# The first k tile loaded as two column halves over the sync and the scalar hardware queue, the offsets moved to the scalar queue

## The chip, the cores and the metric

One core of a Trainium2 chip runs the kernel. The metric is the device time in microseconds (us), of which the profiled span, from the first to the last instruction, is about 1.6 us less. Lower is better.

Names: PE is TensorE, ACT ScalarE, DVE VectorE, POOL GpSimd, SP SyncE. "L53" is line 53 of a kernel's file. DMA queue q0 is POOL's (software descriptors), q1 is SP's and q10 is ACT's (both hardware).

## The reference

For each of 4 batches a window of 64 rows is cut from x at an offset known only at run time, and multiplied with one 4096 x 4096 matrix.

```python
B, S, D, W = 4, 4096, 4096, 64          # x: B,S,D  w: D,D  all float32; offsets: int64
for b in range(B):
    o = int(offsets[b])
    results.append(x[b, o:o+W] @ w)
return np.stack(results).astype(np.float32)
```

So 67.1 MB of w and 4.2 MB of x are read, and 4.2 MB written.

## The kernel before

All of w passes through SBUF once. A DMA issued by POOL reads float32 and writes float16 (`wh`). The first k tile (128 rows of w, 2 MB) goes another way: ACT loads it as float32 over a hardware queue and casts it itself, so that the DMA engines have work from ACT's issue at 0.87 us on, before POOL's first load is issued at 1.38 us. The offsets (32 bytes) come over SP; POOL reads them before it issues the four x loads.

```python
w0_32 = x_pool.tile([P, N], fp32, name="w0row")       # P = 128, N = 4096
w0_16 = x_pool.tile([P, N], fp16, name="w0half")
...
nc.sync.dma_start(out=off_t[:], in_=offsets[None, :])
nc.scalar.dma_start(out=w0_32[:], in_=w[0:P, :])
...
load(0, 1, 1)                                         # first wh tile, gpsimd queue, casts to fp16
make_identity(nc, identity[:])
for b in range(B):                                    # needs the offsets
    g, m = divmod(b, 2)
    o = nc.values_load(off_i32[0:1, 2 * b : 2 * b + 1], engines=[POOL], ...)
    nc.gpsimd.dma_start(out=x16[g][m * WIN : (m + 1) * WIN, :], in_=x[b][bass.ds(o, WIN), :])
for ng in range(n_ng):
    for ki in range(n_k):
        if (ng, ki) not in wh:
            load(ng, ki, 2 if ki < n_k - 4 - (ki % 2) else 1)

nc.scalar.copy(out=w0_16[:, :NG], in_=w0_32[:, :NG])  # NG = 2048
nc.scalar.copy(out=w0_16[:, NG:], in_=w0_32[:, NG:])
... # x transposed on PE; then, per column half, 32 k tiles x 2 row groups x 4 matmuls; results stored
```

Of the kernel before, what the change touches and what calls it, by code (L numbers as in the profile page):

```python
# [1 line left out]

# [5 lines left out]


@with_exitstack  # L10
def kernel(
    ctx: ExitStack,
    tc: tile.TileContext,
    x: bass.AP,
    w: bass.AP,
    offsets: bass.AP,
    out: bass.AP,
):
    nc = tc.nc
    fp32 = mybir.dt.float32  # L20
    fp16 = mybir.dt.float16

    B, S, D = x.shape
    _, N = w.shape
    WIN = out.shape[1]
    P = 128
    NT = 512
    NG = 2048
    n_k = D // P
    n_ng = N // NG  # L30
    n_sub = NG // NT
    G = B // 2

    POOL = mybir.EngineType.Pool

    const_pool = ctx.enter_context(tc.tile_pool(name="const", bufs=1))
    x_pool = ctx.enter_context(tc.tile_pool(name="xp", bufs=1))
    wh_pool = ctx.enter_context(tc.tile_pool(name="wh", bufs=12))
    st_pool = ctx.enter_context(tc.tile_pool(name="st", bufs=1))
    psum_pool = ctx.enter_context(tc.tile_pool(name="ps", bufs=1, space=bass.MemoryType.PSUM))  # L40

    identity = const_pool.tile([P, P], fp16, name="identity")
    off_t = const_pool.tile([1, B], mybir.dt.int64, name="off_t")
    w0_32 = x_pool.tile([P, N], fp32, name="w0row")
    w0_16 = x_pool.tile([P, N], fp16, name="w0half")
    x16 = [x_pool.tile([P, D], fp16, name=f"xrow{g}") for g in range(G)]
    xT = [x_pool.tile([P, D], fp16, name=f"xT{g}") for g in range(G)]
    ps = [psum_pool.tile([P, NT], fp32, name=f"bank{t}") for t in range(8)]

    ctx.enter_context(tc.manual_schedule())  # L50

    nc.sync.dma_start(out=off_t[:], in_=offsets[None, :])
    nc.scalar.dma_start(out=w0_32[:], in_=w[0:P, :])  # L53
    off_i32 = off_t.bitcast(mybir.dt.int32)

    def load(ng, ki, n):
        t = wh_pool.tile([P, n * NG], fp16, name="wh", tag="wh")
        nc.gpsimd.dma_start(  # L58
            out=t[:].rearrange("p (t n) -> p t n", t=n),
            in_=w[ki * P : (ki + n) * P, ng * NG : (ng + 1) * NG].rearrange(  # L60
                "(t p) n -> p t n", p=P
            ),
        )
        for i in range(n):
            wh[(ng, ki + i)] = t[:, i * NG : (i + 1) * NG]

    wh = {(ng, 0): w0_16[:, ng * NG : (ng + 1) * NG] for ng in range(n_ng)}
    load(0, 1, 1)
# [3 lines that stand above are left out]
        o = nc.values_load(  # L72
            off_i32[0:1, 2 * b : 2 * b + 1],
            engines=[POOL],
            min_val=0,
            max_val=S - WIN,
            skip_runtime_bounds_check_because="offsets are drawn below S - WIN",
        )
        nc.gpsimd.dma_start(  # L79
            out=x16[g][m * WIN : (m + 1) * WIN, :],  # L80
            in_=x[b][bass.ds(o, WIN), :]
# [6 lines that stand above are left out]
    nc.scalar.copy(out=w0_16[:, :NG], in_=w0_32[:, :NG])  # L88
    nc.scalar.copy(out=w0_16[:, NG:], in_=w0_32[:, NG:])  # L89
    for g in range(G):  # L90
        for t in range(8):
            for i in range(4):
                k = 4 * t + i
                nc.tensor.matmul(  # L94
                    out=ps[t][:, i * P : (i + 1) * P],
                    lhsT=x16[g][:, k * P : (k + 1) * P],
                    rhs=identity[:],
                    start=True,
                    stop=True,
                )  # L100
            dst = xT[g][:, t * NT : (t + 1) * NT]
            if t % 2 == 0:
                nc.vector.tensor_copy(out=dst, in_=ps[t][:])  # L103
            else:
                nc.scalar.copy(out=dst, in_=ps[t][:])  # L105

    def mm(g, j, ki, rhs, start, stop):
        nc.tensor.matmul(  # L108
            out=ps[4 * g + j][:],
            lhsT=xT[g][:, ki * P : (ki + 1) * P],  # L110
            rhs=rhs,
            start=start,
            stop=stop,
        )

    stage = [
        [st_pool.tile([P, NG], fp32, name=f"stage{ng}{g}") for g in range(G)]
        for ng in range(n_ng)
    ]
    q = [nc.scalar, nc.sync]  # L120
    for ng in range(n_ng):
        last = ng == n_ng - 1
        for ki in range(n_k):
            for g in range(G):
                for j in range(n_sub):
                    mm(g, j, ki, wh[(ng, ki)][:, j * NT : (j + 1) * NT], ki == 0, ki == n_k - 1)
        for j in range(n_sub):
            for g in range(G):
                dst = stage[ng][g][:, j * NT : (j + 1) * NT]
                if g == 0:  # L130
                    nc.scalar.copy(out=dst, in_=ps[4 * g + j][:])  # L131
                else:
                    nc.vector.tensor_copy(out=dst, in_=ps[4 * g + j][:])  # L133
        for g in range(G):
            (q[g] if last else nc.gpsimd).dma_start(  # L135
                out=out[2 * g : 2 * g + 2, :, ng * NG : (ng + 1) * NG],
                in_=stage[ng][g][:],
            )


# [1 line left out]
_INS = ['x', 'w', 'offsets']  # L142
_OUTS = [((4, 64, 4096), 'float32')]


# [23 lines left out]
```

## Time and profile before

| | before |
|---|---|
| device time, median of 6 runs | 183.55 us (183.4 to 183.72) |
| profiled span | 182.0 us |
| DMA time of the queues q0, q10, q1, as shares of 16 engines' span | 97.0 + 4.6 + 1.4 = 103% (the times of packets are added up, and packets of an engine can overlap) |
| HBM traffic over the span | 415 GB/s |
| PE busy | 67% |

The first extract is from the page of before: the DMA row of the 40 slices (tenths of busy time, 9 is 90% or more), the queues (packets, MB, share), the HBM bytes, and the shares of the chain that ended last.

```profile
DMA  5999999999999999999999999999999999999995
...
q0 software_dynamic: 9120, 36.70, 97.0%
q10 hardware_dynamic: 288, 3.15, 4.6%
q1 hardware_dynamic: 146, 1.05, 1.4%
...
HBM read 71.30 MB, written 4.19 MB: 415 GB/s over the span
...
DMA 88%; issue 3%; POOL 1%; DVE 1%; POOLq 1%; PE 1%; DVEq 0%
```

From the second slice to the last but one the DMA engines are busy 90% or more of the time, and the chain is nearly all weight stream. The next extract is from the view of waits (us in total, times, longest; "bank" is a PSUM tile that PE writes, and x is transposed at L94).

```profile
POOL wh L58 <- DMA wh<-in_w_dram: 105.8, 26, 5.8
...
PE bank L108 <- DMA wh<-in_w_dram: 32.7, 30, 1.9
...
PE bank L94 <- DMA xrow<-in_x_dram: 17.5, 2, 16.1
```

PE waits 32.7 us in 30 pieces for weights, and POOL waits 105.8 us for earlier loads to land before it may issue more. Both run behind the DMA engines. The third extract is the timeline (start, duration, instruction, idle before it and what ended it).

```profile
0.87 0.34 SPq L52 DMA_DIRECT2D off_t<-in_offsets_dram  x1
0.87 0.38 ACTq L53 DMA_DIRECT2D w0row<-in_w_dram  x1
...
1.38 0.66 POOL L58 DMA_DIRECT2D wh<-in_w_dram  x1 [0.81 <-POOLq L153]
...
3.54 0.53 POOL L79 DMA_DIRECT2D xrow<-in_x_dram  x1 [0.91 <-issue]
...
9.81 1.90 ACT L88 CAST w0half<-w0row 128x2048 f16<-128x2048 f32 x1 [7.25 <-DMA w0row<-in_w_dram]
...
11.62 1.89 ACT L89 CAST w0half<-w0row 128x2048 f16<-128x2048 f32 x1
...
16.07 3.57 PE L94 MATMUL bank<-identity,xrow 128*128 128x128 f16 x32 [16.07 <-DMA xrow<-in_x_dram]
...
24.41 1.92 PE L108 MATMUL bank<-w0half,xT 128*128 128x512 f16 x8
```

The things to see: the first DMAs are issued at 0.87 us; ACT casts the tile from 9.81 to 13.5 us; PE first uses it at 24.41 us. Between the tile and its use lie 10.9 us in which PE waits for x and then transposes it. Last, from the chain that ended last, the stretch in which the last weight tile lands (start, duration, what):

```profile
145.43 25.79 DMA wh<-in_w_dram
171.22 0.04 issue
```

The last weight tile lands at 171.22 us. What follows it takes 10.8 us to the end of the span: the last matmuls, their copies and the stores.

### The profile page before, as it was taken

The numbers are of one execution on the slowest core, as the hardware profiler recorded it, in microseconds if no ns is written. First come the engines' busy times: TensorE is split into PE (matmuls) and PEld (weight loads), VectorE is DVE, ScalarE is ACT, GpSimd is POOL, SyncE is SP. The second block draws the span as 40 slices with busy tenths as digits, with TensorE's granted clock in tenths as the row PEclk, the third lists the DMA queues.
The fourth block names the chain that finished last, engine by engine and source line by source line (L and its number), as shares of the span: only waits on it lengthen the run. The fifth ranks groups of instructions, "written<-read, shape, count | busy, mean of one in ns | idle before, by whom it ended". The sixth has DMA issues, their size and how long they took to land.

```text
span 182.0 us, 1329 instructions
## 1 busy us (share of the span) xinstructions
PE 122.8 (67%) x576; PEld 56.5 (31%) x576; DVE 10.5 (6%) x16; ACT 13.8 (8%) x19; POOL 27.7 (15%) x48
## 2 busy tenths in 40 slices
PE   0004699777777777777988777777777587799700
PEld 0004663333333322333433333333233232343300
DVE  0002540000000000000005000000000000000040
ACT  2081430000000000000004000000000000000210
POOL 4713310111111111110221111111111010100000
PEclk9999999999999999999999999999999999999995
DMA  5999999999999999999999999999999999999995
GB/s 180 348 217 216 206 214 215 216 214 215 212 213 212 216 215 216 214 215 210 212 214 217 215 215 214 212 214 213 215 216 214 215 215 211 214 212 216 367 398 216
DMA packets 9559, 40.97 MB, mean 225 GB/s; under 512 B 722, under 2 KB 722, under 8 KB 8658
## 3 DMA queue, kind: packets, MB, share of 16 engines
q0 software_dynamic: 9120, 36.70, 97.0%
q10 hardware_dynamic: 288, 3.15, 4.6%
q1 hardware_dynamic: 146, 1.05, 1.4%
q8 instruction: 4, 0.07, 0.1%
q14 instruction: 1, 0.01, 0.0%
HBM read 71.30 MB, written 4.19 MB: 415 GB/s over the span
## 4 chain that ended last, share of the span: by engine, by line
DMA 88%; issue 3%; POOL 1%; DVE 1%; POOLq 1%; PE 1%; DVEq 0%
DMA wh<-in_w_dram 88%; DVE stage L133 1%; POOL wh L58 1%; PE bank L108 1%; POOLq L72 1%; POOL xrow L79 0%; DVEq L164 0%; POOL identity masks.py:197 0%; POOLq L79 0%; POOLq L58 0%; POOLq masks.py:199 0%; POOLq L153 0%
## 5 line engine op out<-in xcount | busy, mean ns | idle before, releaser
L108 PE MATMUL bank<-wh,xT 128*128 128x512 f16 x496 | 112.0, 379 | 32.7 <-DMA wh<-in_w_dram 32.7
L108 PEld LDWEIGHTS <-xT 128*128 128x128 f16 x512 | 49.9, 98 | 98.5 <-issue 42.0
L58 POOL DMA_DIRECT2D wh<-in_w_dram x36 | 23.8, 662 | 116.8 <-DMA wh<-in_w_dram 105.8
L94 PE MATMUL bank<-identity,xrow 128*128 128x128 f16 x64 | 7.1, 311 | 17.5 <-DMA xrow<-in_x_dram 17.5
L131 ACT COPY stage<-bank 128x512 f32<-128x512 f32 x8 | 4.1, 599 | 144.4 <-PE bank L108 144.4
L133 DVE COPY stage<-bank 128x512 f32<-128x512 f32 x8 | 5.0, 682 | 145.1 <-PE bank L108 145.1
L94 PEld LDWEIGHTS <-xrow 128*128 128x128 f16 x64 | 6.7, 147 | 17.7 <-issue 17.7
L103 DVE CAST xT<-bank 128x512 f16<-128x512 f32 x8 | 5.5, 691 | 19.4 <-PE bank L94 19.4
L105 ACT CAST xT<-bank 128x512 f16<-128x512 f32 x8 | 4.7, 586 | 7.0 <-PE bank L94 7.0
L108 PE MATMUL bank<-w0half,xT 128*128 128x512 f16 x16 | 4.2, 380 | 0.2 <-DVE stage L133 0.2
L88 ACT CAST w0half<-w0row 128x2048 f16<-128x2048 f32 x1 | 1.9, 1897 | 7.2 <-DMA w0row<-in_w_dram 7.2
L79 POOL DMA_DIRECT2D xrow<-in_x_dram x4 | 2.1, 524 | 2.1 <-issue 2.1
L135 POOL DMA_DIRECT2D out_dram<-stage x2 | 1.1, 536 | 8.2 <-DMA wh<-in_w_dram 8.2
L89 ACT CAST w0half<-w0row 128x2048 f16<-128x2048 f32 x1 | 1.9, 1892 | 0.0
L88 ACT ACT_TABLE_LOAD x1 | 1.3, 1283 | 1.3 <-PEq L153 1.3
masks.py:199 POOL TENSOR_SCALAR_AFFINE_SELECT identity<-identity 128x128 f16<-128x128 f16 x1 | 0.3, 288 | 0.1
masks.py:197 POOL MEMSET identity<- 128x128 f16 x1 | 0.2, 223 | 0.0
L153 POOL MEMSET const-float32-0.0<- 128x1 f32 x1 | 0.1, 99 | 0.4 <-issue 0.4
L153 POOL MEMSET const-uint8-127<- 128x1 uint8 x1 | 0.1, 102 | 0.0
L153 POOL MEMSET const-bfloat16-1.0<- 128x1 bf16 x1 | 0.1, 101 | 0.0
L153 POOL MEMSET const-float32-1.0<- 128x1 f32 x1 | 0.1, 99 | 0.0
## 6 DMA issues: line engine op xcount, KB each, us to landing
wh<-in_w_dram POOLq DMA_DIRECT2D x26, 1024.0 KB, 36.6
wh<-in_w_dram POOLq DMA_DIRECT2D x10, 512.0 KB, 31.3
w0row<-in_w_dram ACTq DMA_DIRECT2D x1, 2048.0 KB, 8.9
xrow<-in_x_dram POOLq DMA_DIRECT2D x4, 512.0 KB, 12.2
out_dram<-stage POOLq DMA_DIRECT2D x2, 1024.0 KB, 22.8
out_dram<-stage ACTq DMA_DIRECT2D x1, 1024.0 KB, 4.9
out_dram<-stage SPq DMA_DIRECT2D x1, 1024.0 KB, 6.0
off_t<-in_offsets_dram SPq DMA_DIRECT2D x1, 0.0 KB
```

The source lines that it names most:

```text
L58: nc.gpsimd.dma_start(out=t[:].rearrange("p (t n) -> p t n", t=n), in_=w[ki * P : (ki + n) * P, ng * NG : (ng + 1) * NG].rearrange("(t p) ...
L72: o = nc.values_load(off_i32[0:1, 2 * b : 2 * b + 1], engines=[POOL], min_val=0, max_val=S - WIN, skip_runtime_bounds_check_because="offse ...
L79: nc.gpsimd.dma_start(out=x16[g][m * WIN : (m + 1) * WIN, :], in_=x[b][bass.ds(o, WIN), :])
L88: nc.scalar.copy(out=w0_16[:, :NG], in_=w0_32[:, :NG])
L89: nc.scalar.copy(out=w0_16[:, NG:], in_=w0_32[:, NG:])
L94: nc.tensor.matmul(out=ps[t][:, i * P : (i + 1) * P], lhsT=x16[g][:, k * P : (k + 1) * P], rhs=identity[:], start=True, stop=True,)
L103: nc.vector.tensor_copy(out=dst, in_=ps[t][:])
L105: nc.scalar.copy(out=dst, in_=ps[t][:])
L108: nc.tensor.matmul(out=ps[4 * g + j][:], lhsT=xT[g][:, ki * P : (ki + 1) * P], rhs=rhs, start=start, stop=stop,)
L131: nc.scalar.copy(out=dst, in_=ps[4 * g + j][:])
L133: nc.vector.tensor_copy(out=dst, in_=ps[4 * g + j][:])
L135: (q[g] if last else nc.gpsimd).dma_start(out=out[2 * g : 2 * g + 2, :, ng * NG : (ng + 1) * NG], in_=stage[ng][g][:],)
```

## The change

The intent is an earlier start: half of the first tile on each of two queues, so that the first half can be cast sooner, with rows of 8 KB instead of 16 KB. SP has to be free for its half, so the offsets move to ACT, ahead of ACT's half.

```diff
-    nc.sync.dma_start(out=off_t[:], in_=offsets[None, :])
-    nc.scalar.dma_start(out=w0_32[:], in_=w[0:P, :])
+    nc.sync.dma_start(out=w0_32[:, :NG], in_=w[0:P, :NG])
+    nc.scalar.dma_start(out=off_t[:], in_=offsets[None, :])
+    nc.scalar.dma_start(out=w0_32[:, NG:], in_=w[0:P, NG:])
```

## The prediction

> **What bounds the kernel now.** The DMA engines. In the page's slices the DMA row is at 9 (90% or more) from the second slice to the last but one; the queue table adds up to 103% of 16 engines' span; HBM moves 415 GB/s over the 182.0 us span. The chain that ended last is 88% "DMA wh<-in_w_dram", the weight stream on the gpsimd queue. PE waits 32.7 us for that stream. The Trainium skill (DMA: Bandwidth & Descriptors, Measured) lists 425 GB/s for a 16 MB load; this trace's 415 with start and tail included leaves little to gain by moving issues about.
>
> **What the change touches.** The first k tile of w (2 MB, issued by ACT at 0.87 us, landing 8.9 us later) becomes two 1 MB DMAs with 8 KB rows, one on SP and one on ACT; the 32-byte offsets load goes from SP to ACT, ahead of its half. Other engines' order is unchanged. Each ACT cast of the tile now waits for its own half.
>
> Costs, from the DMA records of the trace: in steady state a 16 KB packet of this load takes 0.611 us; the 8 KB packets of the output stores take 0.309 us. So 8 rows per engine cost 4.94 instead of 4.89 us, the same within 0.05. One more DMA issue on ACT costs 0.34 to 0.38 us; ACT has nothing due until the cast at 9.81 us. The Trainium skill (the same page, Issuing engines are not separate DMA queues) says the queues share the same 16 engines. The trace agrees at the end: the SP store, issued at 175.05, begins moving only at 177.1, when ACT's store is through.
>
> **How much lies on the critical path.** The start of the DMA stream does (0.87 issue, first packet 1.89 us, first packets slow, 1.0 to 1.9 us instead of 0.61). An SP issue at 0.87 and smaller rows may start it 0.1 to 0.3 us earlier; ACT's half starts some 0.4 us later, but the engines then have SP's half. The tile's landing does not: both casts end at 13.5 us and the matmuls need w0half first at 24.4 us.
>
> Offsets: the POOL load of them starts at 2.30 us, their packet is at 1.77. If, on ACT, their packet falls behind a first weight packet, they come about 3.1 us, and the four x issues (3.54 to 6.35) shift by up to 1 us. The DMA engines then still have w0 and the first wh tile (3 MB, about 7 us of work), so they don't idle.
>
> **Prediction.** 183.4 us, as before (183.54); 182.8 to 184.1 should hold it 8 times in 10. Faster by over 2%: 0.01; within 2%: 0.98; slower by over 2%: 0.01.
>
> **What would show the steps right or wrong.**
> - Queue table: q10 about 2.1 MB instead of 3.15, q1 about 2.1 instead of 1.05; shares of q1 + q10 about 6.0%, q0 still 97%.
> - The SP half lands early (about 6 to 7 us from the start), the ACT half near 9.5 to 10; first cast starts at about 6.5 instead of 9.81.
> - DMA share 1.0 from 4 us on; HBM rate still 415 GB/s.
> - Last wh landing 171.2 within 0.4; same tail (10.7 us).
>
> **What would make it wrong.** Arbitration that leaves a hole in the gpsimd stream; offsets so late (past 7 us) that the gpsimd queue runs dry; a much slower or faster start of two hardware queues.

## The result and the profile after

| | before | after |
|---|---|---|
| device time, median of 6 runs | 183.55 us | 183.36 us (183.32 to 183.6) |
| ratio, 95% interval | | 0.9993 (0.998 to 1.0005): the same |
| profiled span | 182.0 us | 181.7 us |
| last weight tile landed | 171.22 us | 170.99 us |
| first cast of the first tile starts | 9.81 us | 5.92 us |

The same lines of the page of after:

```profile
DMA  5999999999999999999999999999999999999995
...
q0 software_dynamic: 9120, 36.70, 97.2%
q1 hardware_dynamic: 288, 2.10, 3.1%
q10 hardware_dynamic: 290, 2.10, 2.8%
...
HBM read 71.30 MB, written 4.19 MB: 415 GB/s over the span
...
DMA 89%; issue 3%; POOL 1%; DVE 1%; POOLq 1%; PE 1%; DVEq 0%
```

The bytes have moved from q10 to q1 as the edit says. Nothing else has: q0 has the same 36.70 MB, the rate is 415 GB/s, and the chain is weight stream as before. The waits of after:

```profile
POOL wh L59 <- DMA wh<-in_w_dram: 105.5, 26, 5.3
...
PE bank L109 <- DMA wh<-in_w_dram: 32.5, 29, 2.2
...
PE bank L95 <- DMA xrow<-in_x_dram: 17.8, 2, 16.0
```

They are the same within 0.3 us. The timeline of after:

```profile
0.87 0.51 ACTq L53 DMA_DIRECT2D off_t<-in_offsets_dram  x1
0.87 0.38 SPq L52 DMA_DIRECT2D w0row<-in_w_dram  x1
...
1.41 0.37 ACTq L54 DMA_DIRECT2D w0row<-in_w_dram  x1
...
3.53 0.53 POOL L80 DMA_DIRECT2D xrow<-in_x_dram  x1 [0.91 <-issue]
...
5.92 1.90 ACT L89 CAST w0half<-w0row 128x2048 f16<-128x2048 f32 x1 [2.83 <-DMA w0row<-in_w_dram]
...
10.57 1.90 ACT L90 CAST w0half<-w0row 128x2048 f16<-128x2048 f32 x1 [2.75 <-DMA w0row<-in_w_dram]
...
15.96 3.18 PE L95 MATMUL bank<-identity,xrow 128*128 128x128 f16 x32 [15.96 <-DMA xrow<-in_x_dram]
...
22.79 1.89 PE L109 MATMUL bank<-w0half,xT 128*128 128x512 f16 x8
```

SP's half lands 5.0 us after its issue and is cast at 5.92 us, 3.9 us sooner than before. ACT's half is issued at 1.41 us and lands 9.1 us later; its cast ends at 12.5 us, 1.0 us sooner. None of this reaches the x loads, which are issued at 3.53 us and first used by PE at 15.96 us (before: 3.54 and 16.07). PE does reach the first tile 1.6 us sooner. Nearly all of that is the transposes, which ran at 255 ns each in this profile and at 311 ns in that of before; the change does not touch them, and the repeats have it the other way round (310 ns in e1_again, 262 ns in e9_before_again). PE then waits for the stream anyway. The same stretch of the chain:

```profile
145.20 25.79 DMA wh<-in_w_dram
170.99 0.04 issue
```

The last tile lands 0.23 us sooner, and the tail is 10.7 us.

Where do the 0.2 us come from? The view by windows has these lines for the first 4 us, first of before, then of after (start, end and length of the window, busy us of PE, of its weight loads, of DVE, ACT and POOL, granted clock, DMA share, GB/s; a packet counts in the window in which it starts):

```profile
0.00:2.00 2.00, 0.00 (x0) 0.00 (x0) 0.00 (x0) 0.72 (x1) 0.82 (x5) 1.00 0.34 66
2.00:4.00 2.00, 0.00 (x0) 0.00 (x0) 0.00 (x0) 0.56 (x1) 1.01 (x4) 1.00 0.74 221
```

```profile
0.00:2.00 2.00, 0.00 (x0) 0.00 (x0) 0.00 (x0) 0.19 (x1) 0.82 (x5) 1.00 0.16 33
2.00:4.00 2.00, 0.00 (x0) 0.00 (x0) 0.00 (x0) 1.09 (x1) 1.02 (x4) 1.00 0.91 283
```

Over the two windows the DMA engines are equally busy (0.34 + 0.74 before, 0.16 + 0.91 after), but after moves more in that time: 33 + 283 GB/s against 66 + 221, over 2 us each, are 0.63 MB against 0.57 MB. The stream ramps up faster. In the records of single DMA packets the first packets of w start at the same time (1.89 and 1.88 us). The first 16 KB packets of before take 1.0 to 1.9 us, until they settle at 0.611; the first 8 KB packets of after take 0.47 to 0.96 us, and settle at 0.309. So the first rows are slow with either size, but less time is lost with the smaller one. Whether rows, queues or chance do this is the first question for the experiments; why the much earlier first cast gave nothing is the second.

### The profile page after: what moved, and what is told of

Read it like the earlier page. It is cut to its first block, busy times and chain, and to the rows that moved or that the text cites. A ratio compares the mean times of both kernels' runs of the same rounds, so it can differ in the third digit from the quotient of the medians.

```text
span 181.7 us, 1330 instructions
## 1 busy us (share of the span) xinstructions
PE 122.3 (67%) x576; PEld 55.0 (30%) x576; DVE 10.2 (6%) x16; ACT 13.5 (7%) x19; POOL 27.6 (15%) x48
## 3 DMA queue, kind: packets, MB, share of 16 engines
q0 software_dynamic: 9120, 36.70, 97.2%
## 4 chain that ended last, share of the span: by engine, by line
DMA 89%; issue 3%; POOL 1%; DVE 1%; POOLq 1%; PE 1%; DVEq 0%
DMA wh<-in_w_dram 89%; DVE stage L134 1%; POOL wh L59 1%; PE bank L109 1%; POOLq L73 1%; POOL xrow L80 0%; DVEq L165 0%; POOL identity masks.py:197 0%; POOLq L80 0%; POOLq L59 0%; POOLq masks.py:199 0%; POOLq L154 0%
## 5 line engine op out<-in xcount | busy, mean ns | idle before, releaser
L109 PE MATMUL bank<-wh,xT 128*128 128x512 f16 x496 | 113.5, 383 | 32.5 <-DMA wh<-in_w_dram 32.5
L95 PE MATMUL bank<-identity,xrow 128*128 128x128 f16 x64 | 5.1, 255 | 17.8 <-DMA xrow<-in_x_dram 17.8
L95 PEld LDWEIGHTS <-xrow 128*128 128x128 f16 x64 | 4.8, 118 | 17.9 <-issue 17.9
```

Of the source, the lines that this page charges most:

```text
L95: nc.tensor.matmul(out=ps[t][:, i * P : (i + 1) * P], lhsT=x16[g][:, k * P : (k + 1) * P], rhs=identity[:], start=True, stop=True,)
L109: nc.tensor.matmul(out=ps[4 * g + j][:], lhsT=xT[g][:, ki * P : (ki + 1) * P], rhs=rhs, start=start, stop=stop,)
```

## The experiments

My theory: the 16 DMA engines bound the time from about 2 us on; only bytes, or holes in their stream, change the end. The first tile's landing has slack. Rivals: the landing counts, but what the first half gained was given back by the second; or the start is faster thanks to the second queue; or the difference is noise.

Two quantities, counted from the records of DMA packets of each run, compare the starts: the megabytes read from HBM by 4 us (packets under way counted in part), and the time when the sixth gpsimd load is complete on the median of the 16 engines.

| run | rows of the first tile, queues | read by 4 us | sixth load | median time (ratio) |
|---|---|---|---|---|
| before, first profile | 16 KB, ACT | 0.455 MB | 24.95 us | 183.55 us |
| e9_before_again | 16 KB, ACT | 0.427 MB | 25.11 us | 183.51 us (0.9994) |
| e10_whole_on_sync | 16 KB, SP | 0.437 MB | 25.07 us | 183.55 us (1.0003) |
| after, first profile | 8 KB, SP and ACT | 0.559 MB | 24.78 us | 183.36 us (0.9993) |
| e1_again | 8 KB, SP and ACT | 0.524 MB | 24.82 us | 183.47 us (0.9995) |
| e2_rows_only | 8 KB, ACT twice | 0.541 MB | 24.83 us | 183.44 us (0.9995) |
| e5_cast_late | 8 KB, SP and ACT | 0.510 MB | 24.86 us | 183.44 us (1.0) |
| e4_quarters | 4 KB, SP and ACT twice each | 0.439 MB | 25.36 us | 184.24 us (1.0038) |

### Is the small difference there at all? (e1_again, e9_before_again)

No edit: the changed kernel and the kernel before, each once more.

> The changed kernel once more, beside the same runs of before, to see whether its 0.19 us gain is real. Theory (the DMA stream bounds all; only the start of that stream moved): 183.3 to 183.45 us against 183.55, last weight landing 0.2 us earlier than in before (170.99 against 171.22), all of it present when the first gpsimd weight tile lands (11.2 against 11.35 us, the end of the gpsimd engine's first wait). Rival (the difference is only noise): the medians differ by under 0.1 us or swap.

> The kernel before, unchanged, for a second profile of it and as a measure of the noise. Theory (8 KB rows start the stream about 0.1 us sooner): 183.5 us, about 0.45 MB moved by 4 us and the sixth gpsimd load landing at about 24.95 us at the median engine, as in the first profile of before (0.455 MB, 24.95), outside what the profiles with 8 KB rows show (0.51 to 0.56 MB, 24.78 to 24.86). Rival (start differences are noise): values inside that range.

The repeat of after has 183.47 us (5 runs), that of before 183.51 us, with a ratio of 0.9994 against its own twin runs. The time of the whole kernel therefore cannot resolve the difference: before differs from itself by as much as after does. The traces can. Three profiles with 16 KB rows have the sixth load at 24.95 to 25.11 us, four with 8 KB rows at 24.78 to 24.86 us, and the megabytes of these seven do not overlap either (e8_off_last with 16 KB rows has 0.452 MB, e6_one_half with 8 KB rows 0.521). The means differ by 0.22 us, and by 0.094 MB, which at the steady 428 GB/s is also 0.22 us. (428 GB/s is twice the 214 GB/s of the middle slices, since those count float16 as written.) One of my expectations missed: I wanted the end of POOL's first wait to show it, but that is 11.33 us in e1_again, against 11.35 and 11.23 in the two profiles of before: it scatters by as much as it should have moved. The landing of the last weight tile shows it less clearly too: 170.98 to 171.07 us in the four profiles with 8 KB rows, 171.07 (e10_whole_on_sync), 171.22 and 171.23 in the three with 16 KB rows. That all of the 0.22 us lasts to the end is not shown. The "0.19 us" of the first medians was partly luck; the medians of the later rounds with 8 KB rows differ by 0.07 to 0.1 us.

### Smaller rows or second queue? (e2_rows_only, e10_whole_on_sync, e3_queues_only)

Each run has one part of the change alone.

```diff
 # e2_rows_only, against after: 8 KB rows, one queue
-    nc.sync.dma_start(out=w0_32[:, :NG], in_=w[0:P, :NG])
-    nc.scalar.dma_start(out=off_t[:], in_=offsets[None, :])
+    nc.sync.dma_start(out=off_t[:], in_=offsets[None, :])
+    nc.scalar.dma_start(out=w0_32[:, :NG], in_=w[0:P, :NG])
     nc.scalar.dma_start(out=w0_32[:, NG:], in_=w[0:P, NG:])
 # e10_whole_on_sync, against before: 16 KB rows, queues swapped
-    nc.sync.dma_start(out=off_t[:], in_=offsets[None, :])
-    nc.scalar.dma_start(out=w0_32[:], in_=w[0:P, :])
+    nc.sync.dma_start(out=w0_32[:], in_=w[0:P, :])
+    nc.scalar.dma_start(out=off_t[:], in_=offsets[None, :])
 # e3_queues_only, against after: two queues, row halves, so 16 KB rows
-    nc.sync.dma_start(out=w0_32[:, :NG], in_=w[0:P, :NG])
+    nc.sync.dma_start(out=w0_32[: P // 2, :], in_=w[: P // 2, :])
     nc.scalar.dma_start(out=off_t[:], in_=offsets[None, :])
-    nc.scalar.dma_start(out=w0_32[:, NG:], in_=w[0:P, NG:])
+    nc.scalar.dma_start(out=w0_32[P // 2 :, :], in_=w[P // 2 : P, :])
```

> Column halves with 8 KB rows, but both on the scalar queue; offsets on sync as before. Theory A (the small gain comes from the smaller first packets): as the changed kernel, 183.35 us, first packets 0.5 to 1.0 us long instead of 1.0 to 1.9. Theory B (it comes from the second queue): as before, 183.55 us. Rival of both (the earlier landing of the first half shortens the run): the first cast at about 6 us gives the changed kernel's time in either case.

> The whole tile in 16 KB rows on sync instead of scalar, offsets on scalar: the swap of queues without the split. Theory (row size alone, not the queue, sets the small gain at the start): as before, 183.5 us, 0.43 to 0.47 MB by 4 us, sixth gpsimd load at 24.9 to 25.0. Rival (the sync queue starts faster than the scalar one): 183.35 us and 0.51 MB or more by 4 us.

> Two hardware queues, but row halves (64 rows of 16 KB each), so the packets stay at 16 KB; offsets on scalar. Theory A (small first packets): as before, 183.55 us, first packets 1.0 us or longer. Theory B (two queues): as the changed kernel, 183.35 us.

Rows on one queue (e2_rows_only) start as after does. The other queue without the split (e10_whole_on_sync) starts as before does. So the 0.2 us belong to the row size, and the second queue has no part in them that these runs show. There is one limit to this, in a trace made for another question (e7_off_behind, below): with 8 KB rows and both halves issued at 0.87 us, rows of both queues run mixed from 2.42 us on, and only 0.436 MB have been read by 4 us, as with 16 KB rows. Small rows start sooner where one half goes first, as it does in after (ACT's half begins to move at 4.8 us); why two halves at once lose this is not settled.

The third run went against everything I had expected: 187.5 us, ratio 1.0219 (1.0205 to 1.0233), 4 us slower. Its 16 KB packets took 1.2 to 1.3 us, not 0.61. The lines for 4 to 6 us, first of e3_queues_only, then of after:

```profile
4.00:6.00 2.00, 0.00 (x0) 0.00 (x0) 0.00 (x0) 0.00 (x0) 1.12 (x3) 1.00 1.22 246
```

```profile
4.00:6.00 2.00, 0.00 (x0) 0.00 (x0) 0.00 (x0) 0.08 (x1) 1.11 (x3) 1.00 1.01 395
```

The engines are no less busy than in after and move 246 instead of 395 GB/s in this window (the packets that start in it; some of them end later). So this run says nothing about the two queues at equal speed; it asks a new question.

### Why are row halves slow? (e11_row_halves_one_queue)

```diff
 # against before
     nc.sync.dma_start(out=off_t[:], in_=offsets[None, :])
-    nc.scalar.dma_start(out=w0_32[:], in_=w[0:P, :])
+    nc.scalar.dma_start(out=w0_32[: P // 2, :], in_=w[: P // 2, :])
+    nc.scalar.dma_start(out=w0_32[P // 2 :, :], in_=w[P // 2 : P, :])
```

> Row halves (64 partitions each) as in the run that cost 4 us, but both on the scalar queue, offsets on sync. Theory (a load into 64 partitions [...]runs at half the rate, whatever the queue): 187 to 188 us, 16 KB packets of 1.2 to 1.3 us. Rival (two hardware queues at once with 16 KB rows disturb each other): 183.5 us, packets of 0.61 us.

187.63 us, ratio 1.023, again with long packets (median 1.14 us, and 1.28 us in the first half). The line for 4 to 6 us of e11_row_halves_one_queue:

```profile
4.00:6.00 2.00, 0.00 (x0) 0.00 (x0) 0.00 (x0) 0.00 (x0) 1.12 (x3) 1.00 1.30 262
```

On one queue it is as slow as on two. The shape is what is slow, not the pair of queues. The Trainium skill (SBUF — State Buffer, Door 1: The DMA port swizzle) states that partitions 0 to 63 reach only 8 of SBUF's 16 DMA ports, with an asymptote near 218 GB/s. Our packets agree: the first half, 1.05 MB, moved from 2.19 to 7.24 us in e3_queues_only and from 2.20 to 7.29 us in e11_row_halves_one_queue, at 208 and 206 GB/s. A rival, that reading 64 rows from HBM is slow, finds no support: each x load reads 64 rows of 16 KB too, and writes them as float16 (half the bytes) into 64 partitions, and its packets take 0.624 us in the same two runs. That the ports are the reason is what the skill says; the runs show the rate. Had I read that section before, the result would have been no surprise. It also says why this change was safe: column halves still span all 128 partitions. Had the tile been halved by rows, the same idea would have cost 2%.

### Still smaller rows (e4_quarters)

```diff
 # against after, with H = NG // 2
-    nc.sync.dma_start(out=w0_32[:, :NG], in_=w[0:P, :NG])
+    nc.sync.dma_start(out=w0_32[:, :H], in_=w[0:P, :H])
+    nc.sync.dma_start(out=w0_32[:, H:NG], in_=w[0:P, H:NG])
     nc.scalar.dma_start(out=off_t[:], in_=offsets[None, :])
-    nc.scalar.dma_start(out=w0_32[:, NG:], in_=w[0:P, NG:])
+    nc.scalar.dma_start(out=w0_32[:, NG : NG + H], in_=w[0:P, NG : NG + H])
+    nc.scalar.dma_start(out=w0_32[:, NG + H :], in_=w[0:P, NG + H :])
```

> Four column quarters with 4 KB rows, two on each hardware queue. Theory A (small first packets start the stream sooner): 183.2 to 183.35 us, a further 0.05 to 0.15 us, the first gpsimd weight tile landing before 11.2 us. Theory B (two queues): 183.35, no further gain. If two more issues and 128 more packets cost the engines something: 183.5 or above.

184.24 us, ratio 1.0038 (1.0025 to 1.0052): 0.7 us slower than before. My theory of small first packets fails in this form. By 4 us only 0.439 MB have been read, and by 10 us 2.866 MB against 3.083 in after; the missing 0.217 MB are 0.51 us at 428 GB/s, close to the 0.58 us by which the sixth load is late. Each 4 KB packet takes 0.159 us once settled, little more than half of 0.309; over the 32 packets of an engine that would cost 0.14 us (an estimate). More is lost at the start: 0.120 of the 0.217 MB are missing by 4 us already, before the first row of ACT's half (4.33 us). Why four DMAs of small rows ramp more slowly than two is not settled: I did not separate the number of DMAs from the size of their rows.

### Does the landing of the first tile matter? (e5_cast_late)

```diff
 # against after
-    nc.scalar.copy(out=w0_16[:, :NG], in_=w0_32[:, :NG])
-    nc.scalar.copy(out=w0_16[:, NG:], in_=w0_32[:, NG:])
+    for _ in range(3):
+        nc.scalar.copy(out=w0_16[:, :NG], in_=w0_32[:, :NG])
+        nc.scalar.copy(out=w0_16[:, NG:], in_=w0_32[:, NG:])
```

> The changed kernel with both casts of the first k tile done three times (the same values), so that the last cast ends some 7.6 us later, near 20 us instead of 12.5; ACT's first PSUM casts (17.0 us) move back by about 3 us and the first matmul from 22.8 to 25 us or later. Theory (the landing and casting of this tile has slack, and PE, 67% busy, catches up with the DMA stream): total unchanged within 0.2 us of 183.36. Rival (the landing of the first tile is on the path, and its earlier half was given back by the later one): 2 us or more longer.

183.44 us, ratio 1.0. The timeline of e5_cast_late:

```profile
17.82 1.89 ACT L91 CAST w0half<-w0row 128x2048 f16<-128x2048 f32 x1
...
19.61 2.03 ACT L107 CAST xT<-bank 128x512 f16<-128x512 f32 x4
...
24.49 1.94 PE L110 MATMUL bank<-w0half,xT 128*128 128x512 f16 x8
```

The last cast now ends at 19.7 us, 7.2 us later than in after; ACT's first copy out of PSUM is pushed from 17.0 to 19.6 us, and PE reaches the first tile at 24.49 us. The last weight tile still lands at 170.98 us. The tile may be ready 7 us later for nothing, so its being ready 1 us sooner (its first half 3.9 us sooner) could bring nothing. The rival, a gain given back, falls.

### Do bytes matter? (e6_one_half)

The right half is not loaded, and the left one is cast in its place; the result is wrong.

```diff
 # against after
-    nc.scalar.dma_start(out=w0_32[:, NG:], in_=w[0:P, NG:])
 ...
-    nc.scalar.copy(out=w0_16[:, NG:], in_=w0_32[:, NG:])
+    nc.scalar.copy(out=w0_16[:, NG:], in_=w0_32[:, :NG])
```

> The changed kernel without the scalar half: only the left half is loaded and cast twice, so the result is wrong on purpose; 1.05 MB less to read. Theory (bytes through the 16 DMA engines bound it): shorter by 1.05 MB at the steady 428 GB/s, 2.45 us, so 180.9 us within 0.3, with the last weight landing at about 168.5. Rival (the chain of first loads, casts and matmuls bounds it): less than 1 us shorter.

180.96 us, ratio 0.9863: 2.5 us less for 1.05 MB less, as the stream's rate says (1.05 MB at 428 GB/s are 2.45 us). The line of the chain where the last weight tile has landed, of e6_one_half:

```profile
168.66 0.04 issue
```

It stands at 168.66 us instead of 170.99. Taking 1.05 MB out of the stream shortens the run at the full rate; moving bytes to another queue does not (e10_whole_on_sync).

### Does the place of the offsets matter? (e7_off_behind, e8_off_last)

```diff
 # e7_off_behind, against after
-    nc.scalar.dma_start(out=off_t[:], in_=offsets[None, :])
     nc.scalar.dma_start(out=w0_32[:, NG:], in_=w[0:P, NG:])
+    nc.scalar.dma_start(out=off_t[:], in_=offsets[None, :])
 # e8_off_last, against before
-    nc.sync.dma_start(out=off_t[:], in_=offsets[None, :])
     nc.scalar.dma_start(out=w0_32[:], in_=w[0:P, :])
+    nc.scalar.dma_start(out=off_t[:], in_=offsets[None, :])
```

> The changed kernel with the offsets issued on scalar behind its half instead of ahead of it. Theory: the offsets' packet then stands behind weight packets of its queue and lands at some 5 to 10 us instead of 1.8; the four x issues (3.5 to 6.3 us) shift by as much. If they are issued by about 9 us the DMA engines still have the first weight tiles and the total stays at 183.4; if later, a hole of up to 2 us opens in the DMA row near 10 us and the total grows by the length of the hole, to at most 185.5. Rival (order on a queue is free): offsets at 1.8 us, nothing moves.

> The kernel before, with the offsets on scalar behind the whole 2 MB tile in 16 KB rows (sync issues nothing at the start). Theory: the offsets land with the last rows of the tile or near them (8.5 to 9.5 us), x issues begin at about 10 us, the only other DMA work (the first weight tile) is through by 10 us, so a hole of 1 to 2 us opens and the total grows by as much: 184.5 to 185.7 us. Rival (DMA holes at the start are filled in later, since the average counts): 183.5.

Both are slower, well clear of the noise: 186.94 us (ratio 1.0181, 1.0155 to 1.0207) and 187.0 us (1.0187, 1.017 to 1.0204). The timeline of e7_off_behind:

```profile
0.87 0.38 SPq L52 DMA_DIRECT2D w0row<-in_w_dram  x1
0.88 0.40 ACTq L53 DMA_DIRECT2D w0row<-in_w_dram  x1
1.30 0.54 ACTq L54 DMA_DIRECT2D off_t<-in_offsets_dram  x1
...
11.34 0.53 POOL L80 DMA_DIRECT2D xrow<-in_x_dram  x1 [8.71 <-issue]
```

The offsets' 32-byte packet started at 9.46 us instead of 1.76, behind its queue's weight rows, and the first x load is issued at 11.34 instead of 3.53 us (in e8_off_last 9.07 and 10.96 us). The windows from 10 to 13 us, first of after, then of e7_off_behind:

```profile
10.00:11.00 1.00, 0.00 (x0) 0.00 (x0) 0.00 (x0) 0.43 (x1) 0.00 (x0) 1.00 1.12 229
11.00:12.00 1.00, 0.00 (x0) 0.00 (x0) 0.00 (x0) 1.00 (x1) 0.70 (x1) 1.00 1.02 213
12.00:13.00 1.00, 0.00 (x0) 0.00 (x0) 0.00 (x0) 0.46 (x1) 0.00 (x0) 1.00 1.04 213
```

```profile
10.00:11.00 1.00, 0.00 (x0) 0.00 (x0) 0.00 (x0) 0.82 (x1) 0.00 (x0) 1.00 0.28 53
11.00:12.00 1.00, 0.00 (x0) 0.00 (x0) 0.00 (x0) 1.00 (x2) 0.53 (x1) 1.00 0.00 0
12.00:13.00 1.00, 0.00 (x0) 0.00 (x0) 0.00 (x0) 1.00 (x2) 0.53 (x1) 1.00 0.92 115
```

From 11 to 12 us no DMA engine has work: the first tile and the first gpsimd load are through, and the x loads, which stand next in POOL's order, are not yet there. The gap from the last packet before it to the first after it is about 2.4 us long on a typical engine, and the first x packets are slow again (1.01 us for the first, 0.62 settled). The sixth gpsimd load completes at 28.24 us instead of 24.78, 3.5 us later, and the whole run is 3.6 us longer than after. This hole is not made up for. I had the mechanism right but put the cost at 2 us at most, in both runs; the slow restart and the 3.1 us from the offsets' packet to the first x packet were missing from my sum. This is the one part of the change that could have hurt: the offsets had to be issued ahead of ACT's half, and were.

## Why the prediction was right

The time was predicted as 183.4 us (182.8 to 184.1) and measured as 183.36 us, the same as before. Point by point:

- "The DMA engines" bound the kernel: shown by e6_one_half (bytes taken away shorten the run at 428 GB/s) and by e7_off_behind (a hole lengthens it by its length and the slow restart).
- "The tile's landing does not" lie on the path: shown by e5_cast_late, where 7.2 us of delay cost nothing.
- Two queues share the same engines and give no more rate: shown by e2_rows_only and e10_whole_on_sync, where neither removing nor swapping a queue changed the start, and by e7_off_behind, where both queues move rows at once and the engines move 403 GB/s from 4 to 6 us, against 395 in after. The rate over the span is 415 GB/s in both kernels.
- The start "may start it 0.1 to 0.3 us earlier": the size was right (0.22 us in the traces), but one of the two reasons was wrong. SP's issue at 0.87 us brought nothing, and the first packet came no sooner (1.88 against 1.89 us). The smaller rows did it. And smaller is not always sooner, as e4_quarters and the start of e7_off_behind show.
- The offsets might have landed near 3.1 us behind a weight packet. They did not: their packet started at 1.76 us, and the x issues stayed.
- Landings: the first cast was expected at about 6.5 us and started at 5.92; SP's half was expected at 6 to 7 us and landed at 5.9; ACT's at 9.5 to 10 and landed at 10.5. The two halves did not share the engines evenly. ACT's first weight packet started on each engine only when SP's eight rows there were through, about 2.9 us after SP's first instead of some 0.4. (The records name no engine; but ACT's first packets start at 4.81, 4.84, 4.90 us and so on, 0.01 us behind the 4-byte packets that mark the end of SP's half.) I had read the same of the two stores at the end, and did not carry it over to the start.
- The last weight tile was expected at 171.2 within 0.4 us and landed at 170.99; queue shares were as forecast (3.1 + 2.8 = 5.9% for q1 and q10, 97.2% for q0).

No version tried beats after. The steady stream runs at 428 GB/s, and 75.5 MB at that rate are 176.4 us, an estimate from this trace; with the 1.9 us before the first packet, little but the ramp and the tail is left, as long as all of w is read as float32.

## What to carry to other kernels

When the DMA engines are busy from end to end, splitting a load over more queues moves no bytes sooner; ask instead whether a change takes bytes out or opens a hole, because either goes straight to the total. A load that lands well before its first use is worth nothing more when it lands earlier, and delaying it on purpose is a cheap way to prove that. Keep tiny loads that gate other DMAs at the head of their queue, and halve tiles by columns rather than by partitions.

## What the Trainium skill lacked or had wrong

- DMA: Bandwidth & Descriptors (Rules for kernel authors) says that transfers to disjoint partition halves serialize and are not worth the bother. Here they cost 4 us for a 2 MB tile (187.5 and 187.63 us), since the first half ran at 206 to 208 GB/s (the second ran mixed with POOL's loads). The reason stands only on another page, SBUF — State Buffer (Door 1), with which the runs agree.
- The same page (Queues, rings and completion order) says that an engine takes turns between the queues it has work for, and drains a whole packet, typically 9 to 17 descriptors, from one before it turns to the next. In after, ACT's half, issued 0.54 us behind SP's, started on an engine only when SP's eight rows there were through (first at 4.8 us); that fits if eight rows and their end mark are one such packet. In e7_off_behind, where both were issued at 0.87 us, it does not fit: the rows ran mixed (by 4 us 34 rows of SP's half and 29 of ACT's had started on the 16 engines), and the two halves finished together (the end marks of both come within 0.1 us of each other, between 8.59 and 9.86 us). The page does not say which of the two to expect.
- No page that I found gives the ramp at the start of a stream: the first 16 KB packets took 1.0 to 1.9 us instead of 0.611, the first 8 KB packets 0.47 to 0.96 instead of 0.309, and four DMAs with 4 KB rows had moved less by 10 us (2.866 MB) than two with 8 KB rows (3.083 MB).
- Runtime: NRT & Kernel Launch (Instruction fetch mechanics) says that instructions are fetched in blocks of 16 KiB over a DMA queue and that the cost is mostly hidden; what a fetch takes from a saturated stream, it does not say. Both traces hold four 16 KB packets of the kind "instruction", of 0.89 to 0.98 us each. Around the first, at 30.2 us in before, the spread between the first and the last engine to complete a gpsimd load grew from 0.79 to 1.86 us, and it was still 1.77 us at the end. That the fetch is the cause is read from the trace, and was not tested.
